# Modulation pages, one group at a time, among all the gates of the mixers; padded addends sent by SyncE; small inputs in one DMA

## The chip, the cores and the metric

The kernel runs on one core of a Trainium2 chip. The metric is the device time of one execution in microseconds. The engines are called TensorE (PE in the profile, PEld for its weight loads), VectorE (DVE), ScalarE (ACT), GpSimd (POOL) and SyncE (SP). SyncE only issues DMAs here. ScalarE can issue them too, and its issuing instructions have their own name in the profile, ACTq.

## The reference, cut

The reference is a decoder of two layers with 256 rows of 1024 values. Each layer takes six vectors of 1024 values from the conditioning vector c, and uses them as shift, scale and gate of two halves. The first half has four mixers (S5, sparse attention, RG-LRU, RWKV-7), which a sigmoid gate per channel merges; the second half is a mixture of 16 experts.

```python
def reference(...):
    bsz, seq, d = x.shape
    c_act = jax.nn.silu(c)
    for l in range(DEPTH):
        mod = (c_act @ ada_w[l] + ada_b[l]).reshape(bsz, 6, 1, d)
        shift1, scale1, gate1, shift2, scale2, gate2 = (mod[:, i] for i in range(6))
        h = rmsnorm(x, mix_norm_g[l]) * (1.0 + scale1) + shift1
        u, q, k, v, iq, ik, iw, rg_x, rg_g, rw_f = _split(h @ w_in[l], IN_WIDTHS)
        ...
        branches = jnp.stack([o_s5, o_dsa, o_rg, o_rw], axis=2)
        up = jnp.einsum('btnw,nwd->btnd', branches, branch_w[l])
        gates = jax.nn.sigmoid(h @ gate_w[l] + gate_b[l]).reshape(bsz, seq, N_BRANCH, d)
        mixed = jnp.einsum('btnd,btnd->btd', gates, up) @ out_w[l]
        x = x + gate1 * mixed
        h2 = rmsnorm(x, ffn_norm_g[l]) * (1.0 + scale2) + shift2
        x = x + gate2 * moe(h2, router_w, router_b, exp_w1[l], exp_w3[l], exp_w2[l])
    return rmsnorm(x, final_norm_g)
```

## The kernel before

**Weights** come in pages of 128x2048 f32 (1 MB). One list, `order`, holds all of them in the order in which they are wanted, and SyncE issues them from it, one after the other, whenever one of the five pages of the `ring` (or, at some places, one of the 15 working pages, `page`) comes free (`issue`, L228, and L220 for x and the matrices).

**Modulation.** The six vectors of a layer are made as three groups `(l, g)` of 2048 columns; a group has eight pages, `kt` 0 to 7. Most groups take a page with one ScalarE product (`kt` 0, L486) or four VectorE multiply-adds of 128x512 (L488), and sum over the partitions at the end with ones on TensorE (L494). The two groups in EARLY, (0, 0) and (1, 0), take a page by TensorE alone (L480, four matmuls in the program, eight in the profile), and hold an accumulator bank (`acc`, of which there are three) from their first page to their last. Each group has an addend, `ada_b`: four rows of 512, at the partitions 0, 32, 64 and 96 of a tile that GpSimd sets to zero (L473) before ScalarE issues the DMA (L474). L496 adds it to the sum. `mod_values` then turns the rows into columns (L503 to L525); for g = 2 it also makes the router's scaled weights and their sums (16 small matmuls, L538).

**Mixers.** The mixers are generators that the loop in `_emit` steps in turn, and between their steps it steps `fill`, which walks over the list of `fill_plan(l)`: modulation pages, 16 gate pages and four branch weights. PLAN sets the order of the gates (digits) and branches (letters). A gate page has 48 matmuls of L633 and splits each half of its weights into a high part (ScalarE, L600, `whi`) and a low part (VectorE, L601, `wlo`); projections of the mixers use the same lines. A scheduler then orders the instructions of each engine by priority and readiness, so that the fill lies between the steps of the mixers. What is left of the list when the mixers are through is done behind them, as a tail, with the merges (L1330 to L1336) and the output projection (L1368). Of the S5 scans (L1187 to L1205), each of eight steps has two VectorE products with PSUM (L1191, L1192), two GpSimd additions (L1193, L1194), two VectorE scans (L1196), a VectorE product of two SBUF tiles (L1197) and a GpSimd product (L1198). RG-LRU's own scan comes behind them.

**Start.** The eight pages of group (0, 0) and x come first. ScalarE issues c, and then six DMAs for the small inputs: columns (`cols`, two), positions, frequencies, router bias and router weights. SyncE waits, before it reuses one of the eight DMA semaphores, for the DMA that had it last, whoever issued it.

## Time and profile before

| | before |
|---|---|
| median of 3 runs | 1219.07 us (1212.52 to 1219.73) |
| the profiled execution | 1219.3 us, span 1217.5 us |
| mean granted TensorE clock | 0.948 |
| TensorE busy | 1087.1 us (89%) |
| VectorE busy | 744.1 us (61%) |
| ScalarE, GpSimd busy | 371.2, 230.0 us |
| HBM read | 327.19 MB |
| L488 (VectorE multiply-add of a modulation page) | 112 times, 83.0 us |
| L601 (low half of a weight page) | 122 times, 154.2 us |

The span is cut by stage: the start to about 31 us, the mixers of layer 0 to about 340 and their tail to about 400 us, experts to 640 us, the mixers of layer 1 to about 925 and their tail to about 975 us, then experts and the end. The shares of the whole span are averages over these.

### The profile page before, as it was taken

Reading aid. Unit: us, or ns where it says so; the run is one execution under the profiler, and the core shown is the slowest. Engines: PE = TensorE matmul, PEld = TensorE weight load, DVE = VectorE, ACT = ScalarE, POOL = GpSimd, SP = SyncE. Lnnn points to the kernel's source line nnn. Section 1 sums busy time; section 2 is a strip of 40 time slices with the busy share of each in tenths; the row PEclk is TensorE's granted clock in tenths of the full one; section 3 lists DMA queues with packets and bytes.
Section 4 is the critical chain, followed back from the end, with each engine's and each line's share of the span. In section 5 each row is a group of like instructions: output and inputs, shape, how many; then the busy total and the mean of one; then the engine's idle time right before and its main releaser. Section 6 shows DMA issues by size and latency. Waiting matters only on the chain. (4 is left out here: it accounts for less than half of the span.)

```text
span 1217.5 us, 22749 instructions
## 1 busy us (share of the span) xinstructions
PE 1087.1 (89%) x9286; PEld 701.8 (58%) x9286; DVE 744.1 (61%) x1459; ACT 371.2 (30%) x663; POOL 230.0 (19%) x306
## 2 busy tenths in 40 slices
PE   4878999997988899999887999999898889999995
PEld 0867886865976433433227888987676633343331
DVE  5889995488776322423146889967987642243325
ACT  1643532421643110111016634433254311111112
POOL 0395211034140000009200031004524000000000
PEclk8988998998998899999898999999899989999998
DMA  8724785724566699999773467843156769999883
GB/s 358 280 100 170 281 313 209 310 104 160 221 222 229 244 418 421 419 422 380 298 307 107 171 243 291 300 174 139 40 203 223 295 235 419 420 420 421 357 348 163
DMA packets 47089, 329.82 MB, mean 271 GB/s; under 512 B 5993, under 2 KB 6121, under 8 KB 7553
## 3 DMA queue, kind: packets, MB, share of 16 engines
q1 hardware_dynamic: 45776, 327.47, 69.0%
q8 instruction: 78, 1.28, 0.4%
q10 hardware_dynamic: 1200, 0.79, 0.2%
q14 instruction: 35, 0.28, 0.1%
HBM read 327.19 MB, written 1.05 MB: 270 GB/s over the span
## 5 line engine op out<-in xcount | busy, mean ns | idle before, releaser
L633 PE MATMUL acc<-h_hi,whi 128*128 128x256 f32 x720 | 213.3, 296 | 0.0
L633 PE MATMUL acc<-h_hi,wlo 128*128 128x256 f32 x720 | 206.2, 286 | 5.9 <-DVE wlo L601 5.9
L633 PE MATMUL acc<-h_lo,whi 128*128 128x256 f32 x720 | 205.8, 286 | 0.7 <-DVE h_lo L601 0.7
L600 ACT ACTIVATE whi<-ring 128x1024 fp32r<-128x1024 f32 (+2 forms) x122 | 126.0, 1034 | 205.3 <-PE acc L633 132.7
L601 DVE TENSOR_TENSOR wlo<-ring,whi 128x1024 fp32r<-128x1024 f32 (+2 forms) x122 | 154.2, 1268 | 54.7 <-ACT whi L600 49.9
L633 PEld LDWEIGHTS acc<-h_hi,whi 128*128 128x128 f32 x720 | 139.6, 194 | 17.3 <-issue 10.4
L633 PEld LDWEIGHTS acc<-h_hi,wlo 128*128 128x128 f32 x720 | 139.8, 194 | 9.4 <-DVE wlo L601 7.7
L633 PEld LDWEIGHTS acc<-h_lo,whi 128*128 128x128 f32 x720 | 139.6, 194 | 4.6 <-issue 3.4
L1592 PE MATMUL rw<-page,page 128*32 (+1 forms) x736 | 92.3, 594 | 0.0
L488 DVE SCALAR_TENSOR_TENSOR page<-ring,csil,page 128x512 f32<-128x512 f32 x112 | 83.0, 777 | 1.1 <-DMA ring<-in_ada_w 1.1
L1592 PE MATMUL acc<-page,page 128*32 128x512 f32 (+1 forms) x688 | 82.0, 602 | 0.7 <-DVE page L1536 0.7
L1564 DVE TENSOR_TENSOR page<-page,acc 128x512 f32<-128x512 f32 x64 | 42.3, 684 | 54.8 <-PE acc L1563 54.7
L1614 PE MATMUL mx<-page,page 128*32 128x512 f32 (+1 forms) x560 | 65.7, 607 | 7.0 <-ACT page L1511 6.9
L1623 DVE SCALAR_TENSOR_TENSOR page<-mx,moslw,page 128x512 f32<-128x512 f32 x32 | 24.0, 751 | 74.5 <-PE mx L1614 73.0
L1536 DVE TENSOR_SCALAR page<-mx,scale,shift 128x256 f32<-128x256 f32 x32 | 17.4, 543 | 80.1 <-PE mx L1532 80.0
L600 ACT ACTIVATE wlo<-page 128x512 fp32r<-128x512 f32 x32 | 20.2, 631 | 129.1 <-DVE page L1623 120.0
L1534 ACT ACTIVATE page<-mx,shift,scale 128x256 f32<-128x256 f32 x32 | 18.0, 563 | 124.9 <-PE mx L1532 114.5
L1614 PE MATMUL mx<-ring,page 128*32 (+1 forms) x464 | 54.1, 601 | 0.7 <-ACT page L1511 0.7
L1592 PEld LDWEIGHTS rw<-page,page 128*32 128x32 f32 x736 | 24.4, 110 | 51.4 <-issue 49.5
L1563 PE MATMUL acc<-wlo,whi 128*128 128x512 f32 x128 | 43.6, 438 | 11.0 <-PEq L1602 5.7
L1336 POOL TENSOR_TENSOR page<-page,page 128x512 f32<-128x512 f32 x22 | 33.6, 1547 | 74.9 <-DVE page L1334 74.9
L1592 PEld LDWEIGHTS acc<-page,page 128*32 128x32 f32 x688 | 19.8, 110 | 43.4 <-issue 36.9
(521 smaller groups left out, 2097.8 us busy)
## 6 DMA issues: line engine op xcount, KB each, us to landing
page<-in_w SPq DMA_DIRECT2D x124, 1024.0 KB, 11.9
ring<-in_w SPq DMA_DIRECT2D x68, 1024.0 KB, 10.4
ring<-in_ada_w SPq DMA_DIRECT2D x45, 1024.0 KB, 5.7
ring<-in_gate_w SPq DMA_DIRECT2D x32, 1024.0 KB, 5.0
ring<-in_branch_w SPq DMA_DIRECT2D x8, 1024.0 KB, 4.8
ring<-in_w_rw SPq DMA_DIRECT2D x6, 1024.0 KB, 10.7
ring<-in_w_tm SPq DMA_DIRECT2D x6, 1024.0 KB, 4.8
ring<-in_w_fm SPq DMA_DIRECT2D x6, 1024.0 KB, 4.9
```

The lines of the kernel that those rows point to most:

```text
L488: V.scalar_tensor_tensor(p[:, js], w[:, js], csil[:, kt, 0:1], p[:, js], op0=OP.mult, op1=OP.add)
L600: S.activation(hi, a, AF.Copy)
L601: V.tensor_tensor(lo, a, hi.bitcast(F32), OP.subtract)
L633: PE.matmul(p, w, x_, **f)
L1336: G.tensor_tensor(mix[dp], mix[dp], t, OP.add)
L1534: S.activation(xg[:, kt], p, AF.Identity, scale=sc[:, kt:kt + 1], bias=sh[:, kt:kt + 1])
L1536: V.tensor_scalar(xg[:, kt], p, sc[:, kt:kt + 1], sh[:, kt:kt + 1], op0=OP.mult, op1=OP.add)
L1563: PE.matmul(p, oh[:, P * a:P * a + P], y[:, fs], start=y is yh, stop=y is yl)
L1564: V.tensor_tensor(x[:, a, fs], x[:, a, fs], p, OP.add)
L1592: PE.matmul(hh[f][32 * g:32 * g + 32, :], xg[:, kt, P * i + 32 * g:P * i + 32 * g + 32], w[:, ds(offs[g] + 512 * f, 512)], start=kt == 0, ...
L1614: PE.matmul(yp[f][32 * g:32 * g + 32, :], gT[:, ft, 32 * g:32 * g + 32], w[:, ds(offs[g] + 512 * f, 512)], start=ft == 0, stop=ft == 3)
L1623: V.scalar_tensor_tensor(t, yp[f], o["w"][:, i:i + 1], gate2[:, fs], op0=OP.mult, op1=OP.mult)
```

## The change

Three things change. **The plan:** before, the pages of the groups (l, 1), (l, 2) and, in layer 0, (l + 1, 0) stand in a row, three of them (two in layer 1) ahead of each of the first eight gate pages. After, the eight pages of (l, 1) stand ahead of the gates 0, 0, 1, 2, 3, 4, 5, 6; those of (l, 2) ahead of 7 to 14; those of (l + 1, 0) ahead of 1, 3, ... 15. **The addends** are padded on the host to all 128 partitions (256 KB instead of 8 KB each) and SyncE issues them (L478), with no memset. **The small inputs** come as one array, `par`, 128x420 f32, in one DMA of ScalarE. From here on, lines of the kernel after are 4 to 8 higher than those of before for the same statement.

```diff
+PAR = {}
+_o = 0
+for _n, _w in [("pos", 2), ("freq", 48), ("router_b", NE), ("router_w", KT * NE)] + [(f"cols{l}", NCOL) for l in range(L)]:
+    PAR[_n] = (_o, _w)
+    _o += _w
+NPAR = _o
...
     def fill_plan(l):
 
-        groups = [(l, 1), (l, 2)] + ([(l + 1, 0)] if l + 1 < L else [])
-        adas = [("ada", ll, g, kt) for ll, g in groups for kt in range(KT)]
-        plan, k, ng, seen = [], 0, len(groups), [0] * 4
+        plan, n, seen = [], 0, [0] * 4
         for c in PLAN:
             if c.isdigit():
-                plan += adas[k:k + ng] + [("gate", l, seen[int(c)], int(c))]
-                k += ng
+                for ll, g, at in ((l, 1, (0, 0, 1, 2, 3, 4, 5, 6)), (l, 2, range(7, 15)), (l + 1, 0, range(1, 16, 2))):
+                    if ll < L:
+                        plan += [("ada", ll, g, kt) for kt in range(KT) if at[kt] == n]
+                plan.append(("gate", l, seen[int(c)], int(c)))
+                n += 1
                 seen[int(c)] += 1
             else:
                 plan.append(("br", l, "abcd".index(c)))
...
-    cols = []
-    for l in range(L):
-        c = ct(f"cols{l}", [P, NCOL])
-        nc.scalar.dma_start(c, I["cols"][l])
-        cols.append(c)
+    par = ct("par", [P, NPAR])
+    nc.scalar.dma_start(par, I["par"])
+
+    def of(name, *shape):
+        o, n = PAR[name]
+        a = par[:, o:o + n]
+        return a.rearrange("p (a b) -> p a b", a=shape[0]) if shape else a
+
+    cols = [of(f"cols{l}") for l in range(L)]
...
-    pos_i = ct("pos_i", [P, 2], I32)
-    nc.scalar.dma_start(pos_i, I["pos"])
-    freq = ct("freq", [P, 48])
-    nc.scalar.dma_start(freq, row("freq", 48))
-    rtb = ct("rtb", [P, NE])
-    nc.scalar.dma_start(rtb, row("router_b", NE))
-    rtw = ct("rtw", [P, KT, NE])
-    nc.scalar.dma_start(rtw, I["router_w"])
+    pos_i, freq, rtb, rtw = of("pos").bitcast(I32), of("freq"), of("router_b"), of("router_w", KT)
...
         if kt == 0:
             b = M.take([P, 512])
-            G.memset(b, 0.0)
-            nc.scalar.dma_start(b[0:P:32, :], I["ada_b"][l, g])
+            nc.sync.dma_start(b, I["ada_b"][l, g])
...
-    o["ada_b"] = f("ada_b").reshape(L, 3, 4, 512)
+    o["ada_b"] = np.pad(f("ada_b").reshape(L, 3, 4, 1, 512), [(0, 0)] * 3 + [(0, 31), (0, 0)]).reshape(L, 3, P, 512)
```

SyncE's first issues, with the semaphores that each waits for in brackets: DMAHW0 to DMAHW7 stand for DMAs, PE for TensorE, Activation for ScalarE. Before:

```order
L228 DMA ring_66<-in_ada_w 128x2048
L228 DMA ring_67<-in_ada_w 128x2048
L228 DMA ring_68<-in_ada_w 128x2048 [waits DMAHW1_49]
L228 DMA ring_69<-in_ada_w 128x2048 [waits DMAHW2_49]
L220 DMA page_71<-in_x 128x2x1024 [waits DMAHW3_49]
L228 DMA ring_70<-in_ada_w 128x2048 [waits DMAHW4_49]
L228 DMA page_72<-in_ada_w 128x2048 [waits DMAHW5_49]
L228 DMA page_73<-in_ada_w 128x2048 [waits DMAHW7_49]
L228 DMA page_74<-in_ada_w 128x2048 [waits DMAHW0_49]
L228 DMA ring_66<-in_w_rw 128x2048 [waits DMAHW1_49,PE_49]
```

After:

```order
L236 DMA ring_66<-in_ada_w 128x2048
L236 DMA ring_67<-in_ada_w 128x2048
L236 DMA ring_68<-in_ada_w 128x2048
L236 DMA ring_69<-in_ada_w 128x2048
L228 DMA page_71<-in_x 128x2x1024
L236 DMA ring_70<-in_ada_w 128x2048
L236 DMA page_72<-in_ada_w 128x2048 [waits DMAHW0_49]
L236 DMA page_73<-in_ada_w 128x2048 [waits DMAHW1_49]
L236 DMA page_74<-in_ada_w 128x2048 [waits DMAHW2_49]
L478 DMA page_78<-in_ada_b 128x512 [waits DMAHW3_49,Activation_49]
L236 DMA ring_66<-in_w_rw 128x2048 [waits DMAHW4_49,PE_49]
```

The waits of the third to fifth modulation page and of x are gone, the next three pages wait for c, the first page and the packed input (DMAHW0, 1, 2 in the order of their issue), and the first addend stands ahead of the RWKV weights and waits for ScalarE.

VectorE inside the S5 scans of layer 0 (L1191, L1192, L1196, L1197; after: L1195, L1196, L1200, L1201). Before:

```order
L1196 SCALAR_TENSOR_TENSOR page_75<-s5r,page_72 128x256 x2
L1191 TENSOR_TENSOR page_82<-mx_2953,page_84 128x512
L1197 TENSOR_TENSOR page_72<-page_75,page_84 128x512
L1192 TENSOR_TENSOR page_74<-mx_2953,page_85 128x512
L1334 SCALAR_TENSOR_TENSOR page_72<-page_72,acc_2964 128x512
L1196 SCALAR_TENSOR_TENSOR page_81<-s5r,page_82 128x256 x2
L1191 TENSOR_TENSOR page_80<-mx_2988,page_84 128x512
L1197 TENSOR_TENSOR page_82<-page_81,page_84 128x512
L1192 TENSOR_TENSOR page_80<-mx_2988,page_85 128x512
```

After:

```order
L1195 TENSOR_TENSOR page_75<-mx_2933,page_84 128x512
L1201 TENSOR_TENSOR page_76<-page_81,page_84 128x512
L1196 TENSOR_TENSOR page_83<-mx_2933,page_85 128x512
L492 SCALAR_TENSOR_TENSOR page_78<-ring_69,csil,page_78 128x512
L1200 SCALAR_TENSOR_TENSOR page_80<-s5r,page_75 128x256 x2
L1195 TENSOR_TENSOR page_81<-mx_2962,page_84 128x512
L1201 TENSOR_TENSOR page_75<-page_80,page_84 128x512
L1196 TENSOR_TENSOR page_72<-mx_2962,page_85 128x512
L492 SCALAR_TENSOR_TENSOR page_78<-ring_69,csil,page_78 128x512
L1200 SCALAR_TENSOR_TENSOR page_80<-s5r,page_81 128x256 x2
L492 SCALAR_TENSOR_TENSOR page_78<-ring_69,csil,page_78 128x512
L1201 TENSOR_TENSOR page_81<-page_80,page_84 128x512
```

Multiply-adds of a modulation page (L492 after, L488 before) stand between the scans' steps now. From the first L1191 of a layer to the RG-LRU scan there are 8 of them in layer 0 and 11 in layer 1 (before: none), and 7 and 6 low halves of weights (before: 9 and 8).

TensorE, pages of the early group (1, 0) in layer 0 (L480 before, L484 after). Before:

```order
L987 MATMUL rw_2339<-page_73,page_77 64x64
L990 MATMUL rw_2339<-page_76,page_77 64x64
L480 MATMUL acc_2231<-ring_66,csil 32x512 x4
L480 MATMUL acc_2231<-ring_67,csil 32x512 x4
L480 MATMUL acc_2231<-ring_68,csil 32x512 x4
L633 MATMUL acc_2372<-h_hi,whi_2373 128x256
L633 MATMUL acc_2372<-h_lo,whi_2373 128x256
L633 MATMUL acc_2372<-h_hi,wlo_2374 128x256
```

After:

```order
L1209 MATMUL mx_2714<-page_82,page_73 32x256
L1191 MATMUL mx_2899<-page_82,page_79 128x256 x2
L637 MATMUL acc_2859<-h_hi,whi_2910 128x256
L637 MATMUL acc_2859<-h_lo,whi_2910 128x256
L637 MATMUL acc_2859<-h_hi,wlo_2911 128x256
L484 MATMUL acc_1504<-ring_67,csil 32x512 x4
L637 MATMUL acc_2973<-h_hi,whi_2974 128x256
```

Before, three pages stand in a row, ahead of the S5 scans; after, a page stands between gate matmuls inside them (L1191 is the first product of a scan's step). In layer 0, the matmuls of L633 (1080) fall to 750 ahead of the scans, 112 in them and 218 behind them before, and to 786, 104 and 190 after; in layer 1 to 792, 133 and 155 before, and to 792, 98 and 190 after. Of the early group's eight pages, five stand ahead of the scans, two in them and one behind them (before: all ahead).

## Rows read from the trace of the kernel before

**Rows 1.** Table of windows: PE, PEld, DVE, ACT, POOL busy us; PEclk; DMA share; GB/s.

```profile
140.00:160.00 20.00, 18.16 (x270) 15.77 (x268) 19.81 (x46) 9.76 (x19) 2.41 (x3) 1.00 0.90 356
180.00:220.00 40.00, 36.70 (x327) 27.02 (x325) 23.81 (x51) 9.15 (x19) 5.96 (x9) 0.87 0.67 251
260.00:300.00 40.00, 31.77 (x207) 22.09 (x210) 37.73 (x52) 5.64 (x9) 20.99 (x19) 0.93 0.24 80
840.00:880.00 40.00, 32.69 (x215) 24.56 (x214) 38.12 (x56) 8.35 (x13) 21.00 (x20) 0.87 0.17 64
900.00:920.00 20.00, 18.31 (x126) 16.27 (x124) 16.22 (x17) 9.13 (x13) 5.61 (x4) 1.00 0.32 119
```

**Rows 2.** List of waits on PE, 100 to 200 us: us, times, longest.

```profile
PE mx L503 <- DVE page L496: 3.1, 2, 2.1
PE acc L633 <- DVE wlo L601: 2.2, 3, 1.1
```

**Rows 3.** List of waits on PE, 700 to 800 us.

```profile
PE mx L503 <- DVE page L496: 2.1, 1, 2.1
```

**Rows 4.** Line L488: ns minimum/median/maximum, first and last start.

```profile
L488 DVE SCALAR_TENSOR_TENSOR page<-ring,csil,page x112: 711/740/1652, 108.9 to 789.7; 128x512 f32<-128x512 f32 x112
```

**Rows 5.** List of waits in SyncE's DMA queue, 0 to 60 us.

```profile
SPq L228 <- DMA cols<-in_cols: 2.6, 1, 2.6
SPq L228 <- DMA rtb<-in_router_b: 2.5, 1, 2.5
```

**Rows 6.** Timeline of SyncE's issues at the start: start us, us.

```profile
10.89 3.65 SPq L228 DMA_DIRECT2D page<-in_ada_w  x3
14.66 9.93 SPq L228 DMA_DIRECT2D ring<-in_w_rw  x4
```

**Rows 7.** Table of windows at the start.

```profile
8.00:10.00 2.00, 0.00 (x0) 0.00 (x0) 0.26 (x2) 0.00 (x0) 0.00 (x0) 1.00 0.18 57
10.00:12.00 2.00, 0.64 (x4) 0.20 (x8) 1.02 (x12) 0.00 (x0) 0.00 (x0) 1.00 1.03 425
```

**Rows 8.** DMA page of the first 30 us.

```profile
DMA packets 2580, 10.74 MB, mean 358 GB/s; under 512 B 1037, under 2 KB 1165, under 8 KB 1425
```

**Rows 9.** Timeline of DVE at the start; brackets: idle before, releaser.

```profile
10.97 0.25 DVE L660 TENSOR_SCALAR page<-freq,posf 128x48 f32<-128x48 f32 x1 [1.67 <-DMA freq<-in_freq]
11.14 0.17 DVE L262 TENSOR_SCALAR csil<-cth 128x8 f32<-128x8 f32 x1
...
28.10 0.49 DVE L587 TENSOR_SCALAR page<-page,rstd 128x512 f32<-128x512 f32 x1
31.02 0.69 DVE L496 TENSOR_TENSOR page<-acc,page 128x512 f32<-128x512 f32 x1 [2.43 <-PE acc L480]
```

**Rows 10.** Timeline of PE inside a gate of layer 0.

```profile
183.44 0.28 PE L633 MATMUL acc<-h_hi,whi 128*128 128x256 f32 x1
183.56 0.28 PE L633 MATMUL acc<-h_lo,whi 128*128 128x256 f32 x1
```

**Rows 11.** Timeline of PE: pages of the early group in layer 0.

```profile
189.71 1.02 PE L480 MATMUL acc<-ring,csil 128*32 128x512 f32 x2
...
210.70 2.78 PE L480 MATMUL acc<-ring,csil 128*32 128x512 f32 x24
...
223.33 1.92 PE L480 MATMUL acc<-ring,csil 128*32 128x512 f32 x16
```

**Rows 12.** Groups of DVE, 258 to 300 us: busy us, mean ns.

```profile
L601 DVE TENSOR_TENSOR wlo<-ring,whi 128x1024 fp32r<-128x1024 f32 x4 | 5.4, 1340 | 0.0
```

**Rows 13.** Timeline of DVE in the S5 stretch of layer 0.

```profile
266.47 0.68 DVE L1197 TENSOR_TENSOR page<-page,page 128x512 f32<-128x512 f32 x1
...
271.55 1.45 DVE L1197 TENSOR_TENSOR page<-page,page 128x512 f32<-128x512 f32 x1
```

**Rows 14.** Timeline of POOL in the same stretch.

```profile
271.18 1.27 POOL L1198 TENSOR_TENSOR page<-page,page 128x512 f32<-128x512 f32 x1 [1.88 <-DVE page L1196]
```

**Rows 15.** Timeline of POOL, 640 to 655 us.

```profile
649.48 0.53 POOL L473 MEMSET page<- 128x512 f32 x1 [64.48 <-DVE h_lo L601]
```

More of the change, by code (lines that the diff above doesn't have):

```diff
@@ L1765, in layout @@
     o["x"] = f("x").reshape(T, D)
-    o["pos"] = f("positions").reshape(2, P).T
+    pos = np.ascontiguousarray(f("positions").reshape(2, P).T).astype(np.int32, copy=False)
     o["ada_w"] = f("ada_w").reshape(L, KT, P, 3, 2048).transpose(0, 3, 1, 2, 4)
-    o["ada_b"] = f("ada_b").reshape(L, 3, 4, 512)
+    o["ada_b"] = np.pad(f("ada_b").reshape(L, 3, 4, 1, 512), [(0, 0)] * 3 + [(0, 31), (0, 0)]).reshape(L, 3, P, 512)
     w = f("w_in")
@@ L1793, in layout @@
     o["w2"] = f("exp_w2").reshape(L, 2, NPAIR, 4, P, D).transpose(0, 2, 3, 4, 1, 5).reshape(L, NPAIR, 4, P, 2048)
-    o["router_w"] = f("router_w").reshape(KT, P, NE).transpose(1, 0, 2)
-    o["router_b"] = f("router_b")
     o["final_g"] = f("final_norm_g")
     half = lambda n: np.float32(10000.0) ** (-np.arange(n, dtype=np.float32) / np.float32(n))
-    o["freq"] = np.concatenate([half(32), half(16)]).astype(np.float32)
+    freq = np.concatenate([half(32), half(16)]).astype(np.float32)
     c = np.zeros((L, P, NCOL), np.float32)
@@ L1817, in layout @@
         put(n, f(s))
-    o["cols"] = c
+    rows = lambda a: np.broadcast_to(a[None, :], (P, len(a)))
+    o["par"] = np.concatenate([pos.view(np.float32), rows(freq), rows(f("router_b")),
+                               f("router_w").reshape(KT, P, NE).transpose(1, 0, 2).reshape(P, KT * NE)]
+                              + [c[l] for l in range(L)], axis=1)
     mt = np.zeros((L, P, NMAT), np.float32)
```

## The prediction

> **What bounds the kernel now.** I read the table of 20 and 40 us windows first, since one share for the whole span hides four different stages. In layer 0 the mixers run to about 340 us, in layer 1 from 640 to about 925 us. Before the S5 scans (to about 258 and 838 us) the gates' matmuls keep TensorE nearly full, and VectorE is as full beside it: 18.2 and 19.8 of 20 us at 140 to 160 [rows 1]. TensorE's holes there are waits for VectorE. In layer 0 from 100 to 200 us it waits 3.1 us for the sum of a modulation group (L496) and 2.2 us for the low half of a weight (L601); in layer 1 from 700 to 800 us 2.1 us for L496 [rows 2, 3]. What crowds VectorE is L488, the multiply-add of a modulation page: 112 of them, 740 ns each by the median, the first at 108.9 and the last at 789.7 us [rows 4]; by the order none stands in the S5 stretches. Behind that crowd, at 180 to 220 us, VectorE is busy for only 23.8 of 40 us.
>
> In the S5 stretch the picture turns round. VectorE works 37.7 of 40 us at 260 to 300 and 38.1 at 840 to 880, TensorE only 31.8 and 32.7 [rows 1]: VectorE is what ends last, and gates are filler on TensorE. After it, merges and the rest of the gates run with TensorE at 18.3 of 20 us (900 to 920). The experts move weights and the change does not touch them. At the very start the end is set by the chain page by page: DMA of eight modulation pages, their matmuls, L496.
>
> **The start.** SyncE waits 2.6 us for the columns and 2.5 us for the router's bias before it issues further pages, so that the sixth to eighth page go out only from 10.89 us on [rows 5, 6]. The DMA engines are busy for 0.18 of 8 to 10 us, 1.03 of the next two [rows 7]. In the changed order SyncE has no such wait ahead of the sixth page, so this hole should close: 2 x (1 - 0.18) = 1.6 us. A second piece: SyncE sends the first RWKV weights behind a padded addend, which waits for ScalarE's second square of x. Until the end of the last modulation page these weights now share the engines with it: 10.74 MB moved until 30 us, of which eight pages, x and the small inputs are 9 x 1.05 + 0.23 = 9.67; the other 1.07 MB at 425 GB/s are 2.5 us [rows 7, 8], part of them after that page. I take 1.1 us of it. VectorE is the next that could be late: its chain of tables and norms ends at 28.59, and L496 runs at 31.02, after 2.43 us of waiting for TensorE [rows 9]. That chain begins when the silu of c is done at 11.14, behind an angle that waited until 10.97 for the frequencies; in the new order both angles stand ahead of it and all read the one packed input. It has 215 KB (128 x 420 x 4 bytes) to move beside SyncE's pages; columns, frequencies and positions came between 9 and 11 us by themselves, so I put it at 8 to 11 us, and the chain moves by 0 to -3 us. The start is worth **-2.7 us**, between -4.1 and 0. The other five padded addends are 5 x 256 KB or 3 us of DMA time at 425 GB/s, in stretches where the share is 0.17 to 0.90 [rows 1]: nothing, while there is such room. TensorE's own work there is the same.
>
> **Layer 0, ahead of the S5 scans.** By the order, 12 of 56 multiply-adds leave the stretch, 12 x 0.74 = 8.9 us of VectorE. Of the 3.1 + 2.2 = 5.3 us of waits [rows 2] I give back 4, since the final sum and its waiting transposes remain (those of the second group now come in the tail); bounds 0 and 5.3, and a low clock, which is below, apart. TensorE's filler is also dealt out anew: of 1080 matmuls of L633, 36 more stand ahead of the scans, 8 fewer in them and 28 fewer behind them. A gate matmul comes every 0.12 us [rows 10]. Of the early group (TensorE only) five of eight pages stay ahead of the scans, two move into them and one behind; three pages took 2.78 us, 0.93 each [rows 11]. So TensorE-bound time changes by 36 x 0.12 - 3 x 0.93 = +1.5 ahead and by -28 x 0.12 + 0.93 = -2.4 behind: -0.9 us. This group holds one of the three accumulator banks from the second gate to the sixteenth; before, it ran from 189.71 to past 223.33 us. At 180 to 220 us, with the bank held for most of it, TensorE was busy for 36.7 of 40 us, and the list of waits names no bank [rows 1, 2, 11], so I price the longer hold at nothing. If each of some ten further gates waited 1.1 us for a bank, it would be +11 us.
>
> **The S5 stretch of layer 0.** Between the first S5 product and the RG-LRU scan VectorE has 8 multiply-adds more and 2 weight halves less: 8 x 0.74 - 2 x 1.34 = +3.2 us [rows 4, 12]. Its idle time in 40 us is 40 - 37.7 = 2.3 us, so between +0.9 and +3.2; I take **+2**. The price of one is uncertain here, because GpSimd works in the same stretch for 21 of 40 us [rows 1]. The rows show what happens when both meet: L1197, the same 128x512 product of two SBUF tiles, takes 0.68 us at 266.47 and 1.45 us at 271.55, and a GpSimd product ran from 271.18 to 272.45 beside the second [rows 13, 14]. L488 reads two SBUF tiles too. At 1.45 us each the term is 8 x 1.45 - 2.7 = +8.9. The Trainium skill, SBUF — State Buffer, "Who interferes with whom", says that a VectorE instruction with two SBUF inputs contends with a GpSimd instruction that reads SBUF, and that the one that comes second waits. That speaks against this part of the change, and the two L1197 rows agree with it.
>
> Layer 0 in all: -4 - 0.9 + 2 = **-2.9 us**.
>
> **Layer 1.** Here the plan moves the same 12 multiply-adds, but there is no early group to spread. Ahead of the scans I take -1.6 of 2.1 us [rows 3]. In the S5 stretch 11 more multiply-adds and 2 halves less are 11 x 0.74 - 2.7 = +5.4; with 1.9 us idle, between +3.5 and +5.4 (13.2 at the price of a collision); I take +4.5. Ahead of the scans the number of L633 matmuls is the same (792), 35 leave the scans, and 35 join the tail: 35 x 0.12 = +4.2 us, less what fits into holes of 1.7 in 20 us (900 to 920): I take +2. The matmuls of the second group's values, and of the router sums, move from ahead of the scans to the tail in both layers, from one TensorE-bound stretch to the next: nothing. Layer 1: **+4.9 us**.
>
> **GpSimd and the queues.** The six memsets leave GpSimd, and one of them had made it wait 64.5 us for its page [rows 15]. GpSimd then waited for nothing else, so nothing is gained. Now SyncE has that wait instead, and behind it in its queue stand weights: behind the fifth and sixth addend the second to fourth time-mixing page of layer 1. But the page that they take is another one, freed by work that stands ahead of what these weights serve. I take nothing; a wait that holds SyncE through one gate costs 48 x 0.12 = 5.8 us.
>
> **Sum.** -2.7 - 2.9 + 4.9 = -0.7, on the profiled run's 1219.3 us, which is the median of 1219.07 within 0.3. I say **1218 us**.
>
> **Rivals.** *Unloading VectorE pays more.* In 180 to 220 us the granted clock was 0.87 behind short matmuls and a wait of 2.1 us for L496; a full clock would be worth 0.13 x 40 = 5.2 us [rows 1, 2]. If that dip goes as well and all waits do: -4.1 - (5.3 + 5.2 + 0.9 - 0.9) - 2.1 + 3.5 + 1 = -12.2, 1207 us or less. For it: VectorE is full where the multiply-adds now stand. Against it: TensorE is nearly full there too, and clock dips come wherever TensorE pauses, so that the tail may take this one over.
>
> *The multiply-adds land in the wrong place.* 19 of them now run on the engine that bounds the S5 stretches, beside GpSimd. Without any gain on the waits the sum is 19p - 2 x 2.7 - 0.9 + 4.2 - 1.6, and from p = 0.83 us on it is slower than 1%: at p = 1.1, halfway to a collision each, +17 or 1236 us. Against it: most of L488 ran at 740 ns while GpSimd worked now and then beside it.
>
> *The start does not gain*, because the packed input lands as late as the frequencies did and VectorE's chain ends where it did: 1218 + 2.7 = 1221 us.
>
> **How the numbers follow.** Neutral, as summed, 0.57; more relief 0.18; wrong place 0.13; start without gain 0.12. 1% of this kernel is 12 us, about what its measurement can tell from no change. The first and last case fall within 1%, nearly; the spread of the sum's own terms adds some to either side: faster 0.20, same 0.67, slower 0.13. The range is 1204 to 1232: past the relief's 1207 by some of its unknown clock, and to the lower prices of the collision case.
>
> **What would show it.** Right: a DMA share above 0.9 from 4 to 30 us and L496 before 29 us; fewer L488 before the scans, 8 and 11 in them, and S5 stretches longer by 2 to 5 us; the layer-1 tail longer by about 2. Wrong: L488 above 1 us in the scans, SyncE waiting at the addends, TensorE waiting for an accumulator bank while the early group holds it, or a clock that no longer falls after 180 us.

## The result: 2.45% slower, and the profile after

The changed kernel takes 1248.11 us (median of 4 runs, 1245.27 to 1251.53), the kernel before in the same session 1219.4 us. The ratio is 1.0245 with a 95% interval of 1.0205 to 1.0284. The profiled execution has a span of 1248.8 us at a mean granted clock of 0.943; before, 1217.5 us at 0.948. The range of the prediction ended at 1232 us.

I cut both traces at the same four instructions of a layer: the first projection matmul of the mixers (L635 before, L639 after), the first S5 product on TensorE (L1187, L1191), VectorE's RG-LRU scan (L1273, L1277) and the first matmul of the output projection (L1368, L1372). Their start times, in us from the start of the span:

| | layer 0: projection, S5, RG-LRU scan, output | layer 1: the same | end |
|---|---|---|---|
| before | 57, 249, 325, 356 | 670, 833, 911, 935 | 1217.5 |
| after | 57, 237, 314, 354 | 672, 841, 922, 965 | 1248.8 |

So layer 0 comes out 2 us ahead, with 12 us gained ahead of the scans and 10 lost behind their start. Layer 1 needs 293 in place of 265 us from its projection to its output: 6 more ahead of the scans and 22 more behind their start, 19 of these behind the RG-LRU scan. The rest of the kernel, the experts above all, takes 5 us more; less the 2 that layer 0 gained, this gives the 31 us. Start times are rounded to whole us, so a length can be 1 us off. Below, "ahead" is the stretch from the projection to the first S5 product, "S5 to output" the one from there to the output projection.

**The start** went as forecast. VectorE's first L500 (L496 before), and the windows at 8 and 10 us, as [rows 7, 9] (timeline; then PE, PEld, DVE, ACT, POOL busy, granted clock, DMA share, GB/s):

```profile
28.67 0.69 DVE L500 TENSOR_TENSOR page<-acc,page 128x512 f32<-128x512 f32 x1 [1.70 <-PE acc L484]
```

```profile
8.00:10.00 2.00, 0.00 (x0) 0.00 (x0) 0.73 (x6) 0.00 (x0) 0.00 (x0) 1.00 1.03 432
10.00:12.00 2.00, 1.85 (x12) 0.54 (x16) 2.00 (x28) 0.00 (x0) 0.00 (x0) 1.00 1.01 422
```

The hole is closed (1.03 for 0.18), and the last modulation page is summed at 28.67 for 31.02 us: 2.35 us, of 2.7 forecast. But the first projection matmul starts at 57 us in both kernels, so this gain is gone by then. SyncE did wait at the addends, one of the prediction's signs of being wrong (8.3 us at the first, 6.2 at a later one); what the addends cost is read from h2 below.

**The mixers.** The windows that answer to [rows 1], with one more behind the RG-LRU scan of layer 1:

```profile
180.00:220.00 40.00, 40.00 (x428) 32.66 (x428) 20.94 (x46) 15.80 (x30) 0.58 (x2) 1.00 0.50 184
840.00:880.00 40.00, 33.27 (x229) 25.37 (x228) 35.69 (x56) 6.21 (x10) 18.26 (x19) 0.93 0.22 79
900.00:920.00 20.00, 20.00 (x130) 17.20 (x129) 17.64 (x24) 11.80 (x20) 3.21 (x2) 1.00 0.52 196
920.00:940.00 20.00, 15.09 (x67) 11.93 (x66) 11.69 (x18) 1.06 (x1) 3.33 (x3) 0.66 0.68 262
```

The dip of the clock at 180 to 220 us is gone (1.00 for 0.87). VectorE is busy for 35.7 us of 840 to 880, no more than before. Behind the RG-LRU scan, at 920 to 940 us, TensorE is busy for 15.1 of 20 us at a granted clock of 0.66, between its levels of 1.2 and 2.4 GHz; VectorE and ScalarE (1.1 us) are idle for much of it too. What TensorE does there, and what VectorE does for it:

```profile
920.90 1.06 PE L498 MATMUL acc<-page,ones_f 128*32 128x512 f32 x6
...
927.37 1.92 PE L498 MATMUL acc<-page,ones_f 128*32 128x512 f32 x2 [4.55 <-DVE page L492]
...
930.67 1.05 PE L507 MATMUL mx<-identr,page 128*128 128x128 f32 x4
931.52 3.43 PE L542 MATMUL mx<-page,ones_f 128*128 128x16 f32 x16
```

```profile
916.63 0.75 DVE L492 SCALAR_TENSOR_TENSOR page<-ring,csil,page 128x512 f32<-128x512 f32 x1
...
918.98 1.75 DVE L492 SCALAR_TENSOR_TENSOR page<-ring,csil,page 128x512 f32<-128x512 f32 x1
...
922.19 2.28 DVE L1277 TENSOR_TENSOR_SCAN page<-page,page 128x256 f32<-128x256 f32 x2
...
925.57 1.75 DVE L492 SCALAR_TENSOR_TENSOR page<-ring,csil,page 128x512 f32<-128x512 f32 x1
```

The eighth page of the second group has four multiply-adds (L492) to come on VectorE; they stand one by one between the steps of the RG-LRU branch, and the last runs at 925.57, behind its scan. TensorE waits 4.55 us for it (L498), makes the sum at the low clock, then the transposes (L507) and the router sums (L542, 3.43 us), and only then most of the last two gates (88 of their 96 matmuls), which stand behind in its queue. In the kernel before all of this had ended by 804 us.

**Multiply-adds and waits**, as [rows 4] and [rows 3], and VectorE's groups from the first S5 product to the RG-LRU scan of layer 1, as [rows 12]:

```profile
L492 DVE SCALAR_TENSOR_TENSOR page<-ring,csil,page x112: 720/744/1768, 108.1 to 925.6; 128x512 f32<-128x512 f32 x112
```

```profile
PE mx L1069 <- DVE page L1061: 2.4, 1, 2.4
```

```profile
L1201 DVE TENSOR_TENSOR page<-page,page 128x512 f32<-128x512 f32 x8 | 11.7, 1456 | 0.0
L492 DVE SCALAR_TENSOR_TENSOR page<-ring,csil,page 128x512 f32<-128x512 f32 x11 | 8.9, 832 | 0.0
L605 DVE TENSOR_TENSOR wlo<-ring,whi 128x1024 fp32r<-128x1024 f32 x6 | 7.2, 1214 | 0.1
```

The waits for L496 in that stretch of layer 1 are gone, but a wait of 2.4 us for the rotary product (L1061) has come, and the granted clock ahead of the scans fell from 1.00 to 0.96 (below). In the stretch from the S5 product to the RG-LRU scan, 11 multiply-adds took 832 ns each.

### The profile page after: what moved, and what is told of

Same layout as the page of the kernel before. It is cut to its first block, busy times and chain, and to the rows that moved or that the text cites. A ratio compares the mean times of both kernels' runs of the same rounds, so it can differ in the third digit from the quotient of the medians.

```text
span 1248.8 us, 22724 instructions
## 1 busy us (share of the span) xinstructions
PE 1107.3 (89%) x9286; PEld 718.6 (58%) x9286; DVE 750.2 (60%) x1459; ACT 371.3 (30%) x663; POOL 230.7 (18%) x300
## 5 line engine op out<-in xcount | busy, mean ns | idle before, releaser
L637 PE MATMUL acc<-h_hi,whi 128*128 128x256 f32 x720 | 218.2, 303 | 0.4 <-DVE page L1338 0.4
L637 PE MATMUL acc<-h_hi,wlo 128*128 128x256 f32 x720 | 210.4, 292 | 1.7 <-DVE wlo L605 1.6
L637 PE MATMUL acc<-h_lo,whi 128*128 128x256 f32 x720 | 208.9, 290 | 1.4 <-DVE h_lo L605 1.4
L605 DVE TENSOR_TENSOR wlo<-ring,whi 128x1024 fp32r<-128x1024 f32 (+2 forms) x120 | 148.7, 1240 | 63.3 <-ACT whi L604 62.8
L637 PEld LDWEIGHTS acc<-h_hi,whi 128*128 128x128 f32 x720 | 142.2, 198 | 20.9 <-issue 12.9
L637 PEld LDWEIGHTS acc<-h_hi,wlo 128*128 128x128 f32 x720 | 142.4, 198 | 10.6 <-DVE wlo L605 4.7
L492 DVE SCALAR_TENSOR_TENSOR page<-ring,csil,page 128x512 f32<-128x512 f32 x112 | 89.6, 829 | 7.7 <-DMA ring<-in_ada_w 7.5
L1596 PE MATMUL rw<-page,page 128*32 (+1 forms) x704 | 89.0, 594 | 0.0
L1618 PE MATMUL mx<-ring,page 128*32 x448 | 55.7, 635 | 5.5 <-ACT page L1515 5.5
L1340 POOL TENSOR_TENSOR page<-page,page 128x512 f32<-128x512 f32 x24 | 39.3, 1656 | 107.8 <-DVE page L1338 107.7
```

Source lines behind the costliest of these rows:

```text
L492: V.scalar_tensor_tensor(p[:, js], w[:, js], csil[:, kt, 0:1], p[:, js], op0=OP.mult, op1=OP.add)
L605: V.tensor_tensor(lo, a, hi.bitcast(F32), OP.subtract)
L637: PE.matmul(p, w, x_, **f)
L1340: G.tensor_tensor(mix[dp], mix[dp], t, OP.add)
L1596: PE.matmul(hh[f][32 * g:32 * g + 32, :], xg[:, kt, P * i + 32 * g:P * i + 32 * g + 32], w[:, ds(offs[g] + 512 * f, 512)], start=kt == 0, ...
L1618: PE.matmul(yp[f][32 * g:32 * g + 32, :], gT[:, ft, 32 * g:32 * g + 32], w[:, ds(offs[g] + 512 * f, 512)], start=ft == 0, stop=ft == 3)
```

## The experiments

Five theories stood at the beginning or came on the way. **A:** the second group (l, 2) now ends in the tail, in TensorE's queue ahead of the last gates. **B:** its multiply-adds use up VectorE's time where VectorE bounds. **C:** the addends hold SyncE. **D:** a page takes a step of the fill, so the gates come later. **E:** a late page keeps its ring page too long, and gates leave the scans for that reason. B and E differ in whether the work or the page does it.

All ratios below are against the kernel before on the same chip, with the 95% interval. The stages are read at the four instructions above from one profiled execution of each, so a few us between two rows mean little: the kernels with no late multiply-add (before, e1, e3, h1, h2, i1, i2) differ by up to 5 us in each of the two stretches of layer 1. i2's profiled execution, at 1208.95 us, was its fastest, and its median is 1217.2 us.

| kernel | ratio | layer 0: ahead, S5 to output | layer 1: ahead, S5 to output | of which behind RG-LRU scan, layer 1 |
|---|---|---|---|---|
| before | | 192, 107 | 163, 102 | 24 |
| after | 1.0245 (1.0205 to 1.0284) | 179, 117 | 169, 124 | 43 |
| e1_no_plan | 1.0033 (1.0012 to 1.0055) | 184, 109 | 166, 106 | 27 |
| e2_plan_only | 1.0156 (1.0098 to 1.0214) | 178, 118 | 167, 124 | 43 |
| e3_g2_ahead | 1.0010 (0.9992 to 1.0028) | 181, 109 | 168, 104 | 25 |
| e4_g2_last_late | 0.9990 (0.9974 to 1.0007) | 177, 112 | 160, 106 | 28 |
| f1_light | (below) | 180, 113 | 169, 111 | 32 |
| f2_late_pages | 1.0185 (1.0145 to 1.0226) | 182, 121 | 164, 119 | 38 |
| f3_early_pages | 0.9993 (0.9969 to 1.0017) | 180, 113 | 161, 105 | 26 |
| f4_work_only | 1.0008 (0.9986 to 1.0030) | 173, 119 | 165, 104 | 26 |
| g1_work_in_scans | 1.0178 (1.0129 to 1.0227) | 177, 119 | 162, 123 | 39 |
| g2_late_layer0 | 1.0035 (1.0000 to 1.0069) | 180, 118 | 163, 106 | 28 |
| g3_tensor_pages | 1.0082 (1.0052 to 1.0112) | 177, 114 | 171, 108 | 28 |
| g4_four_late | 1.0064 (1.0035 to 1.0093) | 179, 115 | 167, 110 | 31 |
| h1_packed_only | 1.0031 (1.0017 to 1.0045) | 188, 108 | 166, 106 | 27 |
| h2_addends_only | 1.0008 (0.9990 to 1.0026) | 184, 109 | 163, 107 | 28 |
| h3_early_packed | 1.0008 (0.9986 to 1.0030) | 179, 114 | 163, 106 | 28 |
| h4_faster_fill | 1.0227 (1.0200 to 1.0253) | 179, 116 | 170, 115 | 21 |
| i1_all_early | 0.9998 (0.9978 to 1.0017) | 181, 112 | 166, 105 | 27 |
| i2_early_plan_only | 0.9991 (0.9970 to 1.0011) | 178, 109 | 163, 106 | 26 |

**Which part, and which pages.** e1_no_plan takes `fill_plan` of before into the changed kernel; e2_plan_only takes the new one into the kernel before. The other two change one line of the changed kernel:

```diff
-                for ll, g, at in ((l, 1, (0, 0, 1, 2, 3, 4, 5, 6)), (l, 2, range(7, 15)), ...
+                for ll, g, at in ((l, 1, (0, 0, 1, 2, 3, 4, 5, 6)), (l, 2, range(2, 10)), ...                   # e3_g2_ahead
+                for ll, g, at in ((l, 1, (0, 0, 1, 2, 3, 4, 5, 6)), (l, 2, (0, 1, 2, 3, 4, 5, 6, 14)), ...      # e4_g2_last_late
```

> The changed kernel with the plan of before: only the padded addends on SyncE and the packed small input are new. Theory A (the second group of each layer ends in the tail, and its last multiply-adds, sum, transposes and router sums stand in TensorE's queue there) and theory B (multiply-adds inside the S5 stretch, where VectorE bounds) both put the whole loss into the plan: 1216 to 1217 us, 2 to 3 us below before, from the start. Theory C (SyncE held by the addends, or the addends' bytes): 1225 us or more.

> The kernel before with the new plan alone. A and B: 1249 to 1252 us, the changed kernel plus the 2 to 3 us of the start that it doesn't get. C: 1225 us or less.

> The changed kernel with the pages of group (l, 2) ahead of the gates 2 to 9 in place of 7 to 14. By the order all 56 multiply-adds of a layer and the end of the group then stand ahead of the S5 scans again; in layer 1 the gate matmuls fall as before. A and B: both costs go, 1208 to 1218 us. C: still above 1235.

> The changed kernel with seven pages of group (l, 2) ahead of the gates 0 to 6 and only the last one ahead of gate 14. Gate matmuls fall as in the kernel with the group at 2 to 9; only 4 multiply-adds of a layer stand behind the first scan, but the group's end stands in the tail. A: 1232 to 1248 us, most of the loss. B: a third of the loss or less, 1215 to 1226 us.

The loss is mostly the plan's (C falls): e2 has the stages of the changed kernel from S5 on. But e2 missed its 1249 to 1252 us with 1240.43, and e1 its 1216 to 1217 with 1222.0; the plan alone is 1.0156 and the small parts alone, which were to gain, 1.0033, so the two by themselves add up to some 0.6% less than 1.0245. Why stays open. The plan's loss comes with the late pages of the second group: with them at the gates 2 to 9 it is gone (1219.55 us, just above the range). e4 leaves one page, and so the group's end, at gate 14, and loses nothing either. That speaks against A, but not fully, since with little left to do on VectorE the end came earlier: in the trace its last sum and router sums run ahead of the RG-LRU scan, which starts at 902.49 us:

```profile
897.34 1.06 PE L498 MATMUL acc<-page,ones_f 128*32 128x512 f32 x8 [0.46 <-DVE page L1338]
...
899.51 0.60 PE L507 MATMUL mx<-identr,page 128*128 128x128 f32 x4
899.95 1.86 PE L542 MATMUL mx<-page,ones_f 128*128 128x16 f32 x16
```

So A holds in the changed kernel as a consequence: the end is late because the multiply-adds before it are.

**Work, pages or steps.** f2 and f3 tell the pages from the steps that they take in the fill: f2 has late pages without a step and empty steps early, f3 the reverse.

```diff
-            if key[0] == "ada":
+            if key[0] == "step":
+                yield
+            elif key[0] == "ada":
                 ada(*key[1:])
-                yield
+                if key[1] > l or key[2] != 2:
+                    yield
```

f1 lets VectorE work on 16 of 512 columns in the groups (l, 2), which leaves most of their sums out. f4 takes e4 and adds four multiply-adds ahead of each of the gates 7 to 13 (zero times x, added to the group's sum).

```diff
-                    V.scalar_tensor_tensor(p[:, js], w[:, js], csil[:, kt, 0:1], p[:, js], op0=OP.mult, op1=OP.add)
+                    ls = js if g != 2 else slice(512 * j, 512 * j + 16)                                             # f1
+                    V.scalar_tensor_tensor(p[:, ls], w[:, ls], csil[:, kt, 0:1], p[:, ls], op0=OP.mult, op1=OP.add)
...
+            if key[0] == "spare":                                                                                    # f4
+                p = part[l, 2][1]
+                for j in range(4):
+                    js = slice(512 * j, 512 * j + 512)
+                    V.scalar_tensor_tensor(p[:, js], x[:, j // 2, 512 * (j % 2):512 * (j % 2) + 512], csil[:, 0, 1:2], p[:, js], op0=OP.mult, op1=OP.add)
```

> The changed kernel with the multiply-adds of every second group (l, 2) cut to 16 of 512 columns each, so part of that group's sum is left out; pages, DMAs, fill steps and the group's end stay where the change puts them. Theory A (the end of the group in the tail) is already weak. Theory B (VectorE's time for multiply-adds inside the S5 stretch) and theory E (a late page keeps its ring page until VectorE, which bounds there, has taken it, so that gate matmuls are missing as filler inside the scans and run behind them): 1212 to 1222 us. Theory D (a page takes a step of the fill, so gates are stepped later): 1235 us or more.

> The changed kernel, but the pages of (l, 2) at the gates 7 to 13 take no step of their own in the fill; in their place empty steps stand ahead of the gates 0 to 6, as many as with early pages. B and E: still 1236 us or more. D: 1212 to 1222 us.

> The counterpart: pages of (l, 2) at the gates 0 to 6 without a step, empty steps ahead of the gates 7 to 13, the last page at gate 14. B and E: 1212 to 1222 us. D: 1235 us or more.

> The kernel with seven early pages and the last at gate 14, and ahead of each of the gates 7 to 13 four more multiply-adds of the same shape on VectorE, which add zero times a resident tile to the group's sum (no page, no DMA): 28 more in a layer. By the order the gate matmuls of layer 1 stay at 136 in the scans and 152 behind. B: 1235 us or more. E: 1217 to 1228 us, since VectorE's time alone costs little where it has holes and the gates are not moved.

D falls: f2 is slow, f3 is not. f1's time as a whole tells nothing (4875.72 us: the router gets other values and the experts take another path), but its mixers can be read. Layer 1 needs 111 us from S5 to output, where the changed kernel needs 124: 13 of the 22 us go with the work on VectorE, and 9 stay. f4 did not test what I meant it to: the scheduler put its extra work ahead of the scans in layer 1 (the last at 828.9 us), since nothing held it back. So it shows something else: 28 multiply-adds more there, 19 us of VectorE, cost 5 us of that stretch (165 for 160) and nothing in the median that can be told from no change; in layer 0, where 25 of the 28 stand ahead of the scans, that stretch is even shorter than e4's (173 for 177). These are f4's and e4's windows for it:

```profile
666.00:831.00 165.00, 158.00 (x1801) 143.12 (x1801) 149.07 (x257) 79.47 (x154) 23.68 (x20) 0.99 0.59 212
```

```profile
235.00:347.00 112.00, 102.92 (x684) 78.92 (x683) 92.93 (x130) 36.88 (x56) 40.24 (x35) 0.95 0.49 183
824.00:930.00 106.00, 95.45 (x657) 79.18 (x656) 91.70 (x126) 35.53 (x55) 44.64 (x37) 0.92 0.43 154
664.00:824.00 160.00, 155.40 (x1779) 140.86 (x1778) 130.31 (x229) 79.49 (x152) 21.63 (x19) 1.00 0.59 218
```

**Work inside the scans, without pages.** g1 takes e4 and ties one more multiply-add to each S5 step, which so can't be moved; the other three place late pages differently.

```diff
                 V.tensor_tensor(z, w, csb, OP.mult)
+                js = slice(512 * (j % 4), 512 * (j % 4) + 512)
+                V.scalar_tensor_tensor(part[l, 2][1][:, js], flat(z), csil[:, 0, 1:2], part[l, 2][1][:, js], op0=OP.mult, op1=OP.add)   # g1
...
+  (l, 2, (0, 1, 2, 3, 4, 5, 6, 14) if l else range(7, 15))                                                       # g2_late_layer0
+  (l, 2, range(7, 15) if l else (0, 1, 2, 3, 4, 5, 6, 14)), and EARLY = [(0, 0), (1, 0), (1, 2)]                 # g3_tensor_pages
+  (l, 2, (0, 1, 2, 3, 11, 12, 13, 14))                                                                           # g4_four_late
```

> The kernel with seven early pages and the last at gate 14, with one more multiply-add of the same shape in each of the eight S5 steps of a layer; it adds zero times the step's own tile to the group's sum, so that it must stand inside the scans: 8 more there in each layer, no page, no DMA. Theory B (VectorE's time for multiply-adds in the stretch that it bounds): 8 x 0.75 = 6 us and more in each layer, 1229 us or more. Theory E (a late page keeps its ring page, and gate matmuls go from the scans to the tail): 1217 to 1226 us.

> The changed kernel with late pages of (l, 2) in layer 0 only; layer 1 has seven early ones. If the loss is layer 1's, as the traces of both kernels say (layer 0 ends 2 us earlier there, layer 1 takes 27 us longer): 1219 to 1226 us. If late pages cost the same in each layer: 1230 us or more.

> Late pages of (1, 2) in layer 1, but taken by TensorE alone as an early group, so that a page is free again without VectorE; layer 0 has seven early ones. By the order 141 gate matmuls of layer 1 stand in the scans, 147 behind them. B and E: no loss, 1210 to 1219 us. If late pages cost by their DMAs or by the end of the group in the tail: 1228 us or more.

> The changed kernel with four pages of (l, 2) at the gates 0 to 3 and four at 11 to 14. By the order 133 gate matmuls of layer 1 stay in the scans; 6 multiply-adds stand between the first scan and the RG-LRU scan of layer 1, 12 in layer 0. If the cost is by the multiply-add (B): about half of the loss, 1228 to 1236 us. If it is by the moved gates of layer 1 (E): 1217 to 1226 us.

g1 tells work from pages, and so B from E. Without a page, a DMA or a step, 8 multiply-adds in each layer cost 1.8% more than e4, some 23 us for 16 of them. They took 737 ns each:

```profile
L1203 DVE SCALAR_TENSOR_TENSOR page<-page,csil,page x16: 734/737/742, 242.2 to 887.3; 128x512 f32<-128x512 f32 x16
```

E as the whole cause falls: work alone does it. But in layer 1 the gates moved with it: by the order only 92 L633 matmuls stand in g1's scans there and 196 behind them (e4: 133, 155), and the stretch from S5 to output is 17 us longer than e4's. In layer 0, where they hardly moved (119 and 193; e4: 116, 196), it is 7 us longer. No page stood in the way of the gates; that VectorE's halves of weights come later when VectorE has more to do, and the gates with them, is my reading of it and not shown by itself. The group's end is not told apart by g1 either: its router sums start at 920.1 us, behind the RG-LRU scan at 915.0.

g2 puts most of the loss into layer 1 (1.0035 of 1.0245). g3, without multiply-adds in layer 1's scans, has the stretch from S5 to output at 108 us, near e4's 106, but loses 11 us ahead of the scans: five of its eight pages stand there on TensorE, which is busy for 10 us more than in e4, at a clock of 0.97. Its 1229.85 us lie in the range that I gave to late DMAs or the end of the group, for a reason that none of the theories had. g4 (1226.61 us) lies just above E's range and below B's; its gates in layer 1 stay as in e4 (133, 155), so the moved gates are not what it loses there.

**Gates back into the scans, and the small parts.** h4 keeps the late plan and steps the fill faster; h1 and h2 take one small part each into the kernel before; h3 is e4 with the addends of before.

```diff
-FILL, SPARE = (2, 2, 2, 2, 1, 3, 3), 2
+FILL, SPARE = (2, 2, 2, 2, 2, 4, 4), 2                                                                           # h4_faster_fill
```

> The kernel before with the packed small input alone. If the start's gain of 2 to 3 us is kept to the end: 1215 to 1217 us. If it is lost again before the experts, or by a new order: 1218 us or more.

> The kernel before with the padded addends on SyncE alone. If they are what makes the kernel with both small parts and the plan of before 0.3% slower than before: 1222 to 1226 us, with layer 1 longer by 3 to 6 us. If they are hidden: 1217 to 1220 us.

> Seven early pages of (l, 2) and the last at gate 14, the packed small input, and the addends as before. If the padded addends cost something: 1207 to 1213 us. If not: 1214 to 1218 us as with them.

> The changed kernel with the late plan kept, but the mixers' loop steps the fill 2, 4 and 4 times per round in its last three phases in place of 1, 3 and 3. By the order 11 and 12 multiply-adds stay in the stretch from the S5 scans to the RG-LRU scan, while 144 and 138 L633 matmuls stand in the scans and 144 and 150 behind them (changed kernel: 104 and 98, 190 and 190). If the loss is that gates and the second group's end come behind the RG-LRU scan: 1216 to 1228 us. If VectorE's time for the late multiply-adds is the loss by itself: 1238 us or more.

h4 was 1.0227, in the range for VectorE's time, but its trace divides the loss. The group's end stands ahead of the RG-LRU scan of layer 1 again (its last router sum starts at 918.75, the scan at 933.3 us), and the tail is as short as before's (21 us, 24 before). From S5 to output layer 1 takes 115 us: 9 less than in the changed kernel, with VectorE as busy (98.4 and 97.7 us), and 13 more than before. So of the 22 us some 9 come with the gates and the group's end in the tail, and 13 stay when both are back. What h4 loses besides is elsewhere in its profiled execution: 7 us ahead of the scans of layer 1 (170 for 163), as in the changed kernel, and 7 behind the output projection (289 us to the end, 282 before), which no theory here explains. The windows (layer 0, layer 1, and, for the first two, ahead of the scans of layer 1) of the kernel before, after, of g1 and h4:

```profile
249.00:356.00 107.00, 94.48 (x649) 76.79 (x647) 89.19 (x118) 38.51 (x59) 39.86 (x34) 0.95 0.48 177
833.00:935.00 102.00, 90.33 (x628) 73.87 (x626) 87.94 (x115) 35.78 (x56) 43.09 (x37) 0.93 0.38 136
670.00:833.00 163.00, 154.99 (x1804) 140.05 (x1804) 135.70 (x238) 78.40 (x152) 20.43 (x20) 1.00 0.62 226
```

```profile
237.00:354.00 117.00, 98.22 (x666) 75.43 (x664) 100.13 (x137) 37.30 (x57) 43.11 (x35) 0.99 0.55 205
841.00:965.00 124.00, 102.48 (x643) 83.16 (x639) 97.71 (x133) 35.71 (x55) 41.39 (x34) 0.86 0.39 148
672.00:841.00 169.00, 160.57 (x1795) 146.01 (x1795) 126.54 (x220) 78.41 (x152) 24.05 (x21) 0.96 0.55 199
```

```profile
235.00:354.00 119.00, 99.60 (x685) 78.84 (x684) 100.02 (x138) 36.94 (x56) 42.87 (x35) 0.97 0.47 174
831.00:954.00 123.00, 102.88 (x657) 84.02 (x656) 99.04 (x134) 35.77 (x55) 45.41 (x37) 0.85 0.36 133
```

```profile
237.00:353.00 116.00, 103.27 (x661) 79.74 (x660) 97.21 (x137) 35.97 (x55) 47.18 (x38) 0.91 0.55 207
839.00:954.00 115.00, 100.00 (x632) 81.31 (x630) 98.42 (x133) 35.78 (x55) 43.27 (x34) 0.88 0.48 176
```

Read the third busy time, VectorE's, against the length: 89.2 of 107 and 87.9 of 102 us before; 92.9 of 112 and 91.7 of 106 in e4; 97.2 of 116 and 98.4 of 115 in h4; 100.1 of 117 and 97.7 of 124 after; 100.0 of 119 and 99.0 of 123 in g1. VectorE is busy for 79 to 87% throughout. Against the kernel before, the stretch grew by about 1 us for each us that VectorE had more in layer 0 (10 for 10.9 after), by about 2 in layer 1 (22 for 9.8) and, in h4, whose gates are back in the scans, by 1.2 (13 for 10.5); in g1 against e4 by 7 for 7.1 and 17 for 7.3. The two longest are those with the lowest clock (0.86 and 0.85, layer 1) and with the fewest gate matmuls in the scans (98 and 92).

**A plan with nothing late.**

```diff
-(l, 2, range(7, 15))
+(l, 2, range(0, 8))                 # i1 in the changed kernel, i2 in the kernel before with the new plan
```

> The changed kernel with all pages of (l, 2) ahead of the gates 0 to 7: by the order no multiply-add stands behind the first scan, and the early group stays spread. If each multiply-add between the first scan and the output projection costs what the runs so far say (about 1 us), this is 2 to 4 us below the kernel with the last page at gate 14: 1211 to 1216 us. If only gate matmuls and the granted clock matter: 1216 to 1219 us.

> The same plan on the kernel before, without the packed input and without the padded addends. If the small parts give nothing in the end, the same as with them within 0.3%; if the start's gain counts once nothing else is in the way, 2 to 3 us more than with them.

With no multiply-add behind the first scan the loss is gone, in both. But i1's 1217.06 us lie in the second range: taking e4's last four multiply-adds out as well gains nothing that can be told (e4: 0.9990), so there is no fixed price for each of them. Neither is faster than before: 0.9998 and 0.9991, both intervals hold 1. In i1's trace layer 0 gains 11 us ahead of the scans and keeps 8 of them to its output (348 for 356 us), but its span is only 2 us shorter. No kernel of this study beats the kernel before by more than can be told.

## Why the prediction was wrong

**The step that failed** is the tail, the stretch behind the RG-LRU scan. The prediction cut the mixers there and took the tail for TensorE-bound: -2.4 us in layer 0, and in layer 1 +2, with the second group's values and router sums at nothing, "from one TensorE-bound stretch to the next". Up to the cut it priced nothing too low: from the first S5 product to the RG-LRU scan layer 0 is 1.6 and layer 1 2.2 us longer, for +2 and +4.5. Behind it they are 9.0 and 19.1 us longer. Layer 1, from S5 to the scan and from there to the output, before and after (columns as in [rows 1]):

```profile
832.60:911.30 78.70, 70.51 (x474) 55.83 (x474) 70.78 (x97) 24.97 (x41) 35.77 (x31) 0.91 0.37 134
911.30:935.40 24.10, 20.33 (x159) 18.37 (x157) 17.96 (x19) 11.42 (x15) 8.12 (x6) 1.00 0.42 137
```

```profile
841.30:922.20 80.90, 66.56 (x416) 50.72 (x414) 72.77 (x105) 23.02 (x38) 29.33 (x26) 0.89 0.32 118
922.20:965.20 43.00, 35.61 (x218) 32.19 (x218) 24.93 (x30) 12.87 (x17) 12.26 (x8) 0.80 0.54 208
```

VectorE does 2.0 us more ahead of the scan and 7.0 more behind it, though 11 of the 12 multiply-adds stand ahead: other work went over the cut. The weight halves that I took off went no further than the tail. To the output projection the true addition is 12 multiply-adds in each layer, at 0.74 to 0.99 us by groups, single ones at 1.75; measured by the longer windows above, VectorE has 100.1 - 89.2 = 10.9 us more to do in layer 0 and 97.7 - 87.9 = 9.8 us more in layer 1.

**The 19 us of layer 1's tail** can be taken apart in these rows. TensorE is idle there for 7.4 us in place of 3.8: 3.6 us, the wait of 4.55 us for the last multiply-add above all. It is busy for 15.3 us more: 39 more gate matmuls start behind the scan (96 for 57; 35 were forecast), 4.7 us at 0.12; the group's end (L498, L507, L542 above) is 6.4 us; the rest, some 4 us, has the size of the low clock (0.80 for 1.00) and is not measured apart. The kernel before has the shortest tail of the kernels with nothing late (24 to 28 us), so up to 4 of the 19 us may belong to its one execution. Why layer 1 pays twice what layer 0 does is shown in part by h4: some 9 us go when the gates and the group's end are back.

**Relief ahead of the scans** was -4 and -1.6 us, since VectorE is full there [rows 1]. f4 shows that VectorE's load in that stretch hardly matters: 28 multiply-adds more cost 5 us in layer 1 and none in layer 0, so 12 fewer are worth some 2 by proportion. In layer 0 the stretch did get 13 us shorter, but i1 has all 56 multiply-adds ahead and is 11 us shorter too; e1, with the plan of before, is 8 us shorter. All three have a clock of 1.00 at 180 to 220 us, where the kernel before had 0.87 in its profiled execution; so most of this gain needs no new plan. h1, the other kernel with the plan and the addends of before, has 0.96 and is 4 us shorter; h2, the kernel before with padded addends, has 1.00 and is 8 us shorter. Whether the dip belongs to these kernels or to one execution of each stays open. In layer 1 it got longer, 169 for 163 us at a clock of 0.96 for 1.00; 0.04 x 169 = 6.8 us is that size. It took 160 to 165 us in the kernels with seven pages of (1, 2) at the gates 0 to 6, 163 to 166 with the plan of before or with all eight at the gates 0 to 7, and 164 to 171 in the others. In the changed kernel the clock falls to the lower level three times there, for some 3, 7 and 3 us, each time behind a wait of TensorE (1.3 us at 692.7, the 2.4 for L1061 at 737.7, 1.6 at 834.5). In the kernel before, waits of 1.35, 1.65 and 2.12 us in that stretch were followed by no fall, so what makes it fall stays open.

**The accumulator bank** at nothing, and **the addends** at nothing, were right: the list of TensorE's waits names no bank, and h2 is 1.0008. **The start** was right where it was looked for (2.35 of 2.7 us at L500) and did not last: it was gone by the first projection, and h1, which is the kernel before with a shorter start, is 1.0031 with its interval above 1. h1 is 5 us ahead at layer 0's output and 2 us behind at layer 1's. Why layer 1 is longer there (166 and 106 us for 163 and 102) stays open; its clock at 920 to 940 us was 0.91, 1.00 before.

**The rivals.** The right one was the second, the multiply-adds in the wrong place, with 0.13 and 1236 us. Its place was right. Its mechanism was not: it counted 19 of 24 and expected collisions with GpSimd at 1.1 us each; they ran at 0.74 to 0.83 us in the scans (g1: 0.74), and the loss came behind the scans. That its 1236 us came nearer to the measured time is in part luck. The Trainium skill's rule (SBUF — State Buffer, "Who interferes with whom") was seen in single instructions: the multiply-adds at 918.98 and 925.57 us that took 1.75 us ran beside these GpSimd products (timeline of POOL) and began 0.4 to 0.5 us behind them. In the mean of the scans it was not; the eight multiply-adds there that ran beside a GpSimd instruction began about 0.2 us ahead of it and took 0.72 to 0.74 us:

```profile
916.79 3.39 POOL L1340 TENSOR_TENSOR page<-page,page 128x512 f32<-128x512 f32 x2 [24.09 <-DVE page L1338]
...
925.19 1.57 POOL L1340 TENSOR_TENSOR page<-page,page 128x512 f32<-128x512 f32 x1 [1.27 <-DVE page L1338]
```

## What to carry to other kernels

When work moves from one stretch to another, find how far the second one really goes before you price it: add up the bounding engine's busy time from where it begins to bound to the next point that everything waits for, and count every move across those two ends and none inside. Then ask what the new work pushes out of the stretch and to where, since that is where the time appeared here. A stretch in which one engine is full says little of what unloading it is worth; what is worth something is a wait that ends last, and a kernel with extra work put there (f4, g1) tells that for the price of one run. An item of spread-out work also has an end, with its sums and transposes in another engine's queue: place the end first, and spread the rest ahead of it.

## What was not expected of the hardware

Work can cost more than its own time: 8 multiply-adds of 737 ns, 5.9 us, made layer 1's stretch 17 us longer in g1 (123 for 106), 11 of these behind the RG-LRU scan, with the granted clock at 0.85 for 0.92; 0.07 x 123 = 8.6 us have the size of the clock's part, an estimate that no run measures apart. And one DMA of 210 KB, issued beside six 1 MB DMAs, landed 7.9 us after its issue. VectorE waited for it until 9.13 us, where it had waited for the frequencies until 10.97 before [rows 9]:

```profile
par<-in_par ACTq DMA_DIRECT2D x1, 210.0 KB, 7.9
```
